# Second sequence's mLSTM memory: weighted scores turned by VectorE in 32x32 blocks and a DRAM round trip instead of by TensorE, with the heads interleaved

## The chip, the cores and the metric

The kernel runs on one core of a Trainium2 chip. The metric is the device time of one execution in microseconds (us). A core has several engines that run their own instruction streams side by side: TensorE (PE in the profile, with PEld for its weight loads), VectorE (DVE), ScalarE (ACT), GpSimd (POOL) and SyncE (SP), which here does little but issue DMA transfers. Each stream has a fixed order, set when the kernel is built; an instruction that waits holds up all behind it on its engine. Engines wait for each other through semaphores.

## The reference

One encoder layer is applied to two sequences of 512 tokens with 1024 channels, `x_prompt` (sequence 0) and `x_sample` (sequence 1), each on its own:

```python
def encoder_layer(x, ...):
    x = x + 0.5 * swiglu(rms_norm(x, ffn1_norm), ...)
    h = rms_norm(x, mix_norm)
    aq, ak, av, mq, mk, mv, gate_pre, o_pre, g_att, g_mlstm = split(h @ w_in)
    att = gqa_block_attention(aq, ak, av)
    mem = mlstm_bidirectional(mq, mk, mv, gate_pre, mlstm_gate_bias, o_pre, mlstm_head_norm)
    merged = sigmoid(g_att) * (att @ w_up_att) + sigmoid(g_mlstm) * (mem @ w_up_mlstm)
    x = x + merged @ w_out
    return x + 0.5 * swiglu(rms_norm(x, ffn2_norm), ...)

def mlstm_direction(q, k, v, logi, logf):      # 4 heads of 128 channels; run forward and backward
    ...
        S_qk = einsum('bhtd,bhsd->bhts', qc, kc) * exp(D - m_t[..., None])
        num = einsum('bhts,bhse->bhte', S_qk, vc) + ...
        den = sum(S_qk, axis=-1) + ...
        h = num / maximum(abs(den), exp(-m_t))[..., None]
```

The sum of the two directions is normalized over a head's 128 channels, scaled and gated by `sigmoid(o_pre)`.

## The kernel before

All is float32; a product is three TensorE matmuls of float32r parts: high x high, high x low, low x high (`split`, L715 and L716, makes the parts: ScalarE copies the high one, VectorE subtracts for the low one). After the first feed-forward network, `mix(s, ...)` does the token mixing of sequence s: attention, the mLSTM memory, the merge and the output projection.

The chunked recurrence is computed as one 512x512 matrix of weighted scores per head, both directions in it. For head h:

- `mem_head(h)`: for each of 4 row blocks of 128 queries, three score matmuls into PSUM (L1241), 5 exponentials of 128x128 on ScalarE (L1255; 20 a head) whose rows come from DRAM (`mem_rows`, L1064), a multiplication with a row sum on VectorE (L1257), and, after the denominators (L1261 to L1263), a scaling by them on ScalarE and VectorE (L1268 to L1271). The result `Ts[i][0]` has queries on partitions and keys along the free axis.
- `mem_out(h)`: the product with V needs keys on partitions. So for each of 4 key blocks j, four 128x128 transposes on TensorE (L1283; 16 a head, 64 a sequence) go into a PSUM bank, `split` makes high and low parts in SBUF, and three matmuls (L1291) add into the bank `po` of [channels, queries]. Then square (L1294, ScalarE), gate multiplication (L1296), `block_sums` (L225: VectorE's STREAM_TRANSPOSE, which turns each 32x32 block on its own), a fold matmul (L232), a reciprocal root by small VectorE steps (L235 to L241), spreading (L258), the final multiplication (L1302) and `split` into `mem`.

Other units of work lie between the heads as cover: `mem_qk(h, j)` (query and key projection of a later head), `att_gate` and `mem_gate(d)` (projections of the sigmoid gates, 24 matmuls each on L833; ScalarE's L866 empties the PSUM bank, of which this pool, `mm`, has three), `merge_att(d)` (12 matmuls). `go` runs units and loads the weights of the following ones ahead: sequence 1 reads them from DRAM, where sequence 0 parked them (`w<-wpark`, L293, two SyncE transfers of 512 KB a unit, into a pool of 4 slots). `queue` holds the units that `fill` lets out. The transposed parts, exponentials and other 128x512 work tiles come from one pool (`T2`, tag t2).

Every instruction gets a priority at the place in the code where it is written (`shifted(n)` moves it by n); a scheduler sets each engine's order from these when the kernel is built. In sequence 1 the heads ran one after the other: `mem_head(h)`, one or two units, `mem_out(h)`, more units; after the last head all eight `mem_gate`, then eight `merge_mem`, then the output projection.

Of the kernel before, what the change touches and what calls it, by code (L numbers as in the profile page):

```python
# [8 lines left out]
F32 = mybir.dt.float32  # L9
F32R = mybir.dt.float32r  # L10
I32 = mybir.dt.int32
AF = mybir.ActivationFunctionType
# [4 lines left out]
P = 128  # L17
S = 512
D = 1024
KD = D // P  # L20
# [6 lines left out]
def encoder(ctx, tc, I, outs):  # L27
    nc = tc.nc
    cpool = ctx.enter_context(tc.tile_pool(name="cpool", bufs=1))
    dpool = ctx.enter_context(tc.tile_pool(name="dpool", bufs=1, space=bass.MemoryType.DRAM))  # L30
    apool = ctx.enter_context(tc.tile_pool(name="apool", bufs=7))
    wpool = ctx.enter_context(tc.tile_pool(name="wpool", bufs=3))
# [9 lines left out]
    def nm(s):  # L42
        n_id[0] += 1
        return f"{s}_{n_id[0]}"

    @contextmanager
    def shifted(n):

        tc.cur_priority += n
        yield  # L50
        tc.cur_priority -= n
# [8 lines left out]
    def T2(dtype=F32, tag="t2"):  # L60
        if tag in ("eb", "ac"):
            i = boxes[tag]
            boxes[tag] += 1
            return boxes["tile"][:, i % 4 + (4 if tag == "ac" else 0), :]
        if tag == "R":
            return spool.tile([P, S], dtype, tag="R", bufs=2, name=nm("R"))
        n = {"t2": 11, "f2": 4}[tag]
        return tpool.tile([P, S], dtype, tag=tag, bufs=n, name=nm(tag))
# [41 lines left out]
    def PO():  # L110
        return po_.tile([P, S], F32, tag="o", name=nm("pso"))
# [4 lines left out]
    def PT():  # L116
        return pt.tile([P, S], F32, tag="t", name=nm("pst"))
# [16 lines left out]
    def A(shape, dtype=F32, name="a"):  # L134
        return apool.tile(shape, dtype, tag="a", name=nm(name))
# [85 lines left out]
    def block_sums(t, tag="f2"):  # L221

        row = spool.tile([P, 64], F32, tag="row", bufs=1, name=nm("row"))
        q = T2(F32, tag)
        nc.vector.transpose(q, t)  # L225
        nc.vector.tensor_reduce(row[:, 0:16], q.rearrange("p (n j) -> p n j", j=32), axis=AX.X, op=ALU.add)
        return row

    def block_rstd(row, n, keep=lambda i: i):

        p = PT()
        keep(nc.tensor.matmul(p[:, 0:16], fold, row[:, 0:16], start=True, stop=True))  # L232
        V = nc.vector
        a, y, u = [row[:, 16 * i:16 * i + 16] for i in (1, 2, 3)]
        V.tensor_scalar(a, p[:, 0:16], 1.0 / n, EPS, op0=ALU.mult, op1=ALU.add)  # L235
        V.tensor_scalar(u.bitcast(I32), a.bitcast(I32), 1, None, op0=ALU.logical_shift_right)
        V.tensor_scalar(y.bitcast(I32), u.bitcast(I32), -1.0, 1597463007.0, op0=ALU.mult, op1=ALU.add)
        for _ in range(3):
            V.scalar_tensor_tensor(u, y, -0.5, y, op0=ALU.mult, op1=ALU.mult)
            V.tensor_tensor(u, u, a, op=ALU.mult)  # L240
            V.scalar_tensor_tensor(y, u, 1.5, y, op0=ALU.add, op1=ALU.mult)  # L241
        return y
# [13 lines left out]
    def spread_rows(r16, R):  # L256

        nc.vector.transpose(R.rearrange("p (n j) -> p n j", j=32), r16.unsqueeze(2).to_broadcast([P, 16, 32]))  # L258
        return R
# [48 lines left out]
    V_ = nc.vector  # L308
# [404 lines left out]
    def split(src, hi, lo, eng=None):  # L713

        nc.scalar.activation(hi, src, AF.Copy)  # L715
        (eng or V_).tensor_tensor(lo, src, f(hi), op=ALU.subtract)  # L716
# [3 lines left out]
    HM, DM = 4, 128  # L720
# [50 lines left out]
    def go(*units):  # L771
        for load, comp in units:
            held.append((comp, load()))
            while len(held) > ahead[0]:
                c, w = held.pop(0)
                c(w)
# [64 lines left out]
    def mix(s, xh, xl, early=None, extra=None, after=None):  # L841
# [3 lines left out]
        queue = []  # L845

        def fill(n):
            go(*queue[:n])
            del queue[:n]

        def F2(dtype=F32):
            return T2(dtype, "f2")
# [10 lines left out]
        def gate_of(t, p):  # L863
            if not s:
                V_.tensor_tensor(t, p, R[s], op=ALU.mult)
            nc.scalar.activation(t, t if not s else p, AF.Tanh, scale=0.5)  # L866

        def win_cols(c0, done):
            return proj(win_v[:, :, c0:c0 + P], ("in", c0), xsrc, KD, done)
# [128 lines left out]
        def mem_values():  # L998
            def done(pvv):
                vm = A([P, 2, 4, S], F32R, "Vm")  # L1000
                for b in range(4):
                    nc.scalar.activation(vm[:, 0, b, :], pvv[b], AF.Copy, scale=rcol(b))
                    rest(vm[:, 1, b, :], pvv[b], b, f(vm[:, 0, b, :]))
                Vm.append(vm)
            return tok_proj(xh, xl, [(1792, 512)], 2, done, (MM, MM, MM, PO))
# [3 lines left out]
        def mem_qk(h, j):  # L1009
            def done(pp):  # L1010
                if j == 0 and not s:
                    t = wpool.tile([P, 4, S], F32R, tag="w8", bufs=4, name=nm("qk"))
                    qks[h] = [t[:, i] for i in range(4)]
                elif s:
                    t = wpool.tile([P, 2, S], F32R, tag="wr", bufs=4, name=nm("qk"))
                    qks.setdefault(h, []).extend(t[:, i] for i in range(2))
                t = pp
                if not s:
                    t = F2()
                    V_.tensor_tensor(t, pp, R[s], op=ALU.mult)  # L1020
                split(t, *qks[h][2 * j:2 * j + 2])
            return win_cols((768, 1280)[j] + h * P, done)

        ogs = {}
# [136 lines left out]
        for h in range(HA):  # L1161
            nxt = []
# [43 lines left out]
        def merge_att(d):  # L1206
            def done(pu):
                V_.scalar_tensor_tensor(mg[:, d, :], mg[:, d, :], 1.0, pu, op0=ALU.add, op1=ALU.mult)
            return up_unit(0, d, att, done)
# [3 lines left out]
        def mem_gate(d):  # L1213
            def done(pp):
                t = ths[d] = T2()
                gate_of(t, pp)
            return win_cols(3856 + d * P, done)
# [11 lines left out]
        mem = A([P, HM, 2, S], F32R, "mem")  # L1229

        def mem_head(h):
# [39 lines left out]
                    V_.tensor_scalar(tf[:, up_], tb[:, up_], rb, None, op0=ALU.mult)  # L1271
            return Ts

        def mem_out(h, Ts):
            vm = Vm[0]
            po = PO()
            hs_ = slice(h * P, (h + 1) * P)
            turned = []
            for j in range(4 + 1):
                if j < 4:  # L1280
                    p = PT()
                    for i in range(4):
                        nc.tensor.transpose(p[:, i * P:(i + 1) * P], Ts[i][0][:, j * P:(j + 1) * P], ident)  # L1283
                    ph, pl = T2(F32R), T2(F32R)
                    split(p, ph, pl)
                    turned.append((j, ph, pl))
                if j >= 1:
                    t, ph, pl = turned.pop(0)
                    with shifted(15):
                        for n, (a, b) in enumerate(((0, ph), (1, ph), (0, pl))):  # L1290
                            nc.tensor.matmul(po, vm[:, a, t, hs_], b, start=(t == 0 and n == 0),  # L1291
                                             stop=(t == 3 and n == 2))
            h2 = T2()
            nc.scalar.activation(h2, po, AF.Square)  # L1294
            og = ogs[h]
            V_.scalar_tensor_tensor(og, og, 1.0, po, op0=ALU.add, op1=ALU.mult)  # L1296
            row = block_sums(h2)
            with shifted(60):
                rh = block_rstd(row, DM)
            with shifted(160):  # L1300
                Rh = spread_rows(rh, T2(F32, "f2"))
                V_.scalar_tensor_tensor(og, og, hn[:, h:h + 1], Rh, op0=ALU.mult, op1=ALU.mult)  # L1302
                split(og, mem[:, h, 0, :], mem[:, h, 1, :])

        for h in range(HM):
            Ts = mem_head(h)
            if h == 0:
                go(*mem_values())
            queue.append(merge_att(2 * h))
            if h == 0:  # L1310
                queue.append(merge_att(1))
            fill(1 + s)
            mem_out(h, Ts)
            if h + 2 < HM:
                queue.extend([att_gate(h + 6), mem_qk(h + 2, 0), mem_qk(h + 2, 1)])
            if h:
                queue.append(merge_att(2 * h + 1))
            fill(99)

        mh, ml = A([P, KD, S], F32R, "mh"), A([P, KD, S], F32R, "ml")  # L1320
        go(*[mem_gate(d) for d in range(KD)])
        go(*[merge_mem(d) for d in range(KD)])
        flush()
        yield None
# [22 lines left out]
    def busy(n, idle):  # L1347

        for _ in range(n):
# [3 lines left out]
    x2buf = [dpool.tile([P, KD, S], F32, name=f"x2buf{s}") for s in range(2)]  # L1353
    rbuf = [[[dpool.tile([P, 2, S], F32, name=f"rbuf{n}_{j}_{m}") for m in range(7)] for j in range(NF // 2)]
            for n in range(2)]
    xnbuf = dpool.tile([P, KD, S], F32, name="xnbuf")
    raws = [A([P, 4, D], F32, "raw")]
    x0r_ = A([P, KD, S], F32, "x0r")
# [288 lines left out]
    r = [None, None]  # L1647
# [213 lines left out]
```

## Time and profile before

| | |
|---|---|
| runs, us | 2044.56, 2046.38, 2044.59; median 2044.59 |
| profiled execution: own time / span, us | 2046.24 / 2044.5 |
| mean granted TensorE clock | 0.999 |
| TensorE busy, us (share of the span) | 2034.3 (100%) |
| VectorE / ScalarE / GpSimd busy, us | 1571.5 / 909.1 / 93.6 |
| DMA, mean | 218 GB/s, 445.38 MB |
| second sequence's memory: first transpose to last product matmul | 1208.3 to 1287.4 us |

Matmuls overlap their neighbours in the pipeline, so that the recorded duration of one (0.39 us for 128x512) is longer than the time from its start to the next one's. "Idle before" and the waits name the instruction that ended the idle time. A group row reads: line, engine, operation, output<-inputs, count, busy us, mean ns of one, idle time before.

### The profile page before, as it was taken

To read this page: it belongs to the slowest core of one execution; us is meant where nothing else is said; L and a number is where in the kernel's file an instruction comes from. 1 tells how busy PE (TensorE), PEld (TensorE's weight loads), DVE (VectorE), ACT (ScalarE), POOL (GpSimd) and SP (SyncE) were. 2 spreads that over 40 slices of the span, in tenths; PEclk is the share of its full clock that TensorE was granted. 3 is DMA by queue.
4 is the path that set the end of the run, shared out by engine and by line. 5 is a ranking of instruction groups with operands and counts; after the bars stand their busy time and mean duration, and the time that the engine had idled before them with its cause. 6 is when DMAs were issued, how large, how long until landed. Compare 5 with 4: busy or idle time off the path is not lost.

```text
span 2044.5 us, 26753 instructions
## 1 busy us (share of the span) xinstructions
PE 2034.3 (100%) x9313; PEld 1680.7 (82%) x9313; DVE 1571.5 (77%) x2780; ACT 909.1 (44%) x1655; POOL 93.6 (5%) x116
## 2 busy tenths in 40 slices
PE   9999999999999999999999999999999999999998
PEld 7888888888888888888888888888888888888887
DVE  7988888886797798786567756366788988786797
ACT  7644444443234577563325554144444444442224
POOL 0000000001003000100120000001000000000001
PEclk9999999999999999999999999999999999999999
DMA  9656566799766853868564345667655655699753
GB/s 308 199 172 224 172 213 187 236 338 362 270 215 223 293 173 130 284 211 292 188 195 139 114 152 169 226 202 225 192 190 181 207 170 180 203 347 341 275 198 119
DMA packets 314727, 445.38 MB, mean 218 GB/s; under 512 B 19848, under 2 KB 189920, under 8 KB 313312
## 3 DMA queue, kind: packets, MB, share of 16 engines
q1 hardware_dynamic: 312512, 437.69, 63.8%
q0 software_dynamic: 1920, 5.72, 0.9%
q8 instruction: 73, 1.20, 0.2%
q14 instruction: 62, 0.51, 0.1%
q10 hardware_dynamic: 160, 0.27, 0.0%
HBM read 284.06 MB, written 159.55 MB: 217 GB/s over the span
## 4 chain that ended last, share of the span: by engine, by line
PE 96%; DVE 2%; ACT 1%; DMA 1%; issue 0%; SPq 0%; DVEq 0%; ACTq 0%
PE mm L833 15%; PE pst L374 12%; PE pso L374 12%; PE mm L374 10%; PE mm L632 8%; PE pss L374 6%; PE mm L820 5%; PE pst L632 4%; PE pss L632 4%; PE mm L800 4%; PE pso L632 3%; PE pso L1121 1%; PE pss L1094 1%; PE pst L1110 1%; PE pso L1291 1%; PE pss L1241 1%
## 5 line engine op out<-in xcount | busy, mean ns | idle before, releaser
L374 PE MATMUL pst<-xc,w 128*128 128x512 f32 x1056 | 253.7, 389 | 0.0
L374 PEld LDWEIGHTS pst<-xc,w 128*128 128x128 f32 x1056 | 198.2, 188 | 41.2
L374 PE MATMUL mm<-xc,w 128*128 128x512 f32 x972 | 229.7, 390 | 0.4 <-ACT f L382 0.4
L374 PEld LDWEIGHTS mm<-xc,w 128*128 128x128 f32 x972 | 182.0, 188 | 38.4 <-ACT f L382 0.8
L632 PE MATMUL mm<-rt,w 128*128 128x512 f32 x765 | 178.7, 389 | 0.0
L833 PE MATMUL mm<-xh,w 128*128 128x512 f32 x560 | 176.9, 392 | 0.0
L632 PEld LDWEIGHTS mm<-rt,w 128*128 128x128 f32 x765 | 143.5, 188 | 29.8
L332 ACT ACTIVATE w<-t 128x512 fp32r<-128x512 f32 x176 | 106.6, 627 | 135.6 <-issue 63.1
L333 DVE TENSOR_TENSOR w<-t,w 128x512 fp32r<-128x512 f32 x176 | 117.8, 687 | 42.9 <-ACT w L332 41.2
L374 PE MATMUL pss<-xc,w 128*128 128x512 f32 x528 | 126.8, 389 | 0.0
L374 PE MATMUL pso<-xc,w 128*128 128x512 f32 x528 | 126.8, 389 | 0.0
L374 PE MATMUL pso<-xc,f 128*128 128x512 f32 x528 | 126.8, 389 | 0.0
L833 PEld LDWEIGHTS mm<-xh,w 128*128 128x128 f32 x560 | 104.9, 188 | 21.9
L374 PEld LDWEIGHTS pss<-xc,w 128*128 128x128 f32 x528 | 99.1, 188 | 20.6
L374 PEld LDWEIGHTS pso<-xc,w 128*128 128x128 f32 x528 | 99.1, 188 | 20.6
L374 PEld LDWEIGHTS pso<-xc,f 128*128 128x128 f32 x528 | 99.1, 188 | 20.6
L820 PE MATMUL mm<-xh,w 128*128 128x512 f32 x336 | 113.4, 400 | 0.0
L833 PE MATMUL mm<-xl,w 128*128 128x512 f32 x280 | 109.6, 391 | 0.0
L715 ACT ACTIVATE w<-wr 128x512 fp32r<-128x512 f32 x72 | 45.1, 632 | 136.7 <-PE pso L632 71.2
L278 ACT ACTIVATE w<-wr 128x1024 fp32r<-128x1024 f32 (+1 forms) x64 | 65.3, 1029 | 79.1 <-issue 23.7
L279 DVE TENSOR_TENSOR w<-wr,w 128x1024 fp32r<-128x1024 f32 (+1 forms) x64 | 79.7, 1247 | 26.5 <-ACT w L278 15.7
L715 ACT ACTIVATE w<-t 128x512 fp32r<-128x512 f32 x82 | 51.8, 632 | 107.6 <-PE pst L632 62.5
(444 smaller groups left out, 4068.7 us busy)
## 6 DMA issues: line engine op xcount, KB each, us to landing
rt<-rbuf SPq DMA_DIRECT2D x154, 512.0 KB, 5.5
wpark<-w SPq DMA_DIRECT2D x88, 512.0 KB, 3.8
w<-wpark SPq DMA_DIRECT2D x88, 512.0 KB, 4.4
wr<-in_ffn_w_gate_dram SPq DMA_DIRECT2D x62, 512.0 KB, 5.3
rbuf<-tab SPq DMA_DIRECT2D x102, 256.0 KB, 4.0
wr<-in_ffn_w_up_dram SPq DMA_DIRECT2D x44, 512.0 KB, 4.5
rbuf<-f SPq DMA_DIRECT2D x72, 256.0 KB, 4.0
wr<-in_w_in_dram SPq DMA_DIRECT2D x36, 512.0 KB, 5.7
```

The costliest lines, as they stand in the source:

```text
L278: pin(nc.scalar.activation(hi, raw, AF.Copy))
L279: pin(lo_eng.tensor_tensor(lo, raw, f(hi), op=ALU.subtract))
L332: pin(nc.scalar.activation(t[:, 0], src, AF.Copy))
L333: pin(V_.tensor_tensor(t[:, 1], src, f(t[:, 0]), op=ALU.subtract))
L374: nc.tensor.matmul(p, a[:, k, :], xt[:, b, k, :], start=(first and k == 0 and i == 0), stop=(k == HK_ - 1 and i == 2), skip_group_check=True)
L632: nc.tensor.matmul(p, u[:, a, d * P:(d + 1) * P], r[:, b, ts], start=(first and q == 0 and k == 0), stop=(q == len(us) - 1 and k == 2), sk ...
L715: nc.scalar.activation(hi, src, AF.Copy)
L800: nc.tensor.matmul(p[b][:, :N], a[:, k, bs], w_[:, kl, :], start=(k == 0 and i == 0), stop=(k == KD - 1 and i == 2))
L820: pin(nc.tensor.matmul(p[0], a[:, k, :], b, start=(k == 0 and i == 0), stop=(k == n - 1 and i == 2)))
L833: nc.tensor.matmul(p, a[:, k, :], b, start=(k == 0 and i == 0), stop=(k == n - 1 and i == 2))
L1094: pin(nc.tensor.matmul(p, qT[:, h, b * P:(b + 1) * P], kv[:, hk * 2 + j, :], start=(j == 0), stop=(j == 1)))
L1110: pin(nc.tensor.transpose(p[:, b * P:(b + 1) * P], Ps[b][:, kb * P:(kb + 1) * P], ident))
```

## The change

Only sequence 1 changes (`if s`). `mem_blocks(h, Ts)` turns the weighted scores by 8 VectorE STREAM_TRANSPOSEs of 128x256 (L1279) into two tiles `q` of the `wr` pool (named `qt`), and writes them by 8 SyncE transfers of 128 KB in runs of 512 bytes (L1283) into one of two DRAM buffers `tbuf`. `mem_out` reads key block j back by one transfer of 256 KB (L1295) into a t2 tile, which `split` takes instead of a PSUM bank; TensorE's transposes are gone there. The columns come back in another order, so ScalarE copies `po` with the order undone (L1314) ahead of the square (L1317); L1318 and L1324 are the former L1296 and L1302, L1308 the former L1291, and L1299 the former L1283 (sequence 0 only).

`mem_head(h + 1)` and its blocks now stand ahead of `mem_out(h)`. The queue's order is another one: `mem_gate(0)` to `mem_gate(2)` are put in during head 2 and so run ahead of and between the products of heads 2 and 3. Head 2's query and key parts lie in a part of `mem` instead of the `wr` pool.

```diff
@@ -1012,7 +1012,7 @@
                     t = wpool.tile([P, 4, S], F32R, tag="w8", bufs=4, name=nm("qk"))
                     qks[h] = [t[:, i] for i in range(4)]
                 elif s:
-                    t = wpool.tile([P, 2, S], F32R, tag="wr", bufs=4, name=nm("qk"))
+                    t = mem[:, 2 + j] if h == 2 else wpool.tile([P, 2, S], F32R, tag="wr", bufs=4, name=nm("qk"))
                     qks.setdefault(h, []).extend(t[:, i] for i in range(2))
                 t = pp
                 if not s:
@@ -1271,16 +1271,33 @@
                     V_.tensor_scalar(tf[:, up_], tb[:, up_], rb, None, op0=ALU.mult)
             return Ts
 
+        def mem_blocks(h, Ts):
+
+            q = [wpool.tile([P, 8, 4, 32], F32, tag="wr", bufs=4, name=nm("qt")) for _ in range(2)]
+            for i in range(4):
+                for g in range(2):
+                    V_.transpose(q[g][:, :, i, :],
+                                 Ts[i][0][:, g * 256:(g + 1) * 256].rearrange("p (n m) -> p n m", m=32))
+            for g in range(2):
+                for a in range(4):
+                    nc.sync.dma_start(tbuf[h % 2][8 * g:8 * g + 8, :, a, :].rearrange("n r x -> r n x"),
+                                      q[g][32 * a:32 * a + 32].rearrange("r n i m -> r n (i m)"))
+            return h % 2
+
         def mem_out(h, Ts):
             vm = Vm[0]
             po = PO()
             hs_ = slice(h * P, (h + 1) * P)
             turned = []
             for j in range(4 + 1):
-                if j < 4:
+                if j < 4 and s:
+                    p = T2()
+                    nc.sync.dma_start(p, tbuf[Ts][4 * j:4 * j + 4].rearrange("c r a x -> (c r) (a x)"))
+                elif j < 4:
                     p = PT()
                     for i in range(4):
                         nc.tensor.transpose(p[:, i * P:(i + 1) * P], Ts[i][0][:, j * P:(j + 1) * P], ident)
+                if j < 4:
                     ph, pl = T2(F32R), T2(F32R)
                     split(p, ph, pl)
                     turned.append((j, ph, pl))
@@ -1291,8 +1308,13 @@
                             nc.tensor.matmul(po, vm[:, a, t, hs_], b, start=(t == 0 and n == 0),
                                              stop=(t == 3 and n == 2))
             h2 = T2()
+            og = ogs[h]
+            if s:
+                rows_ = T2()
+                nc.scalar.activation(rows_.rearrange("p (i a m) -> p i a m", i=4, a=4),
+                                     po.rearrange("p (a i m) -> p i a m", i=4, a=4), AF.Copy)
+                po = rows_
             nc.scalar.activation(h2, po, AF.Square)
-            og = ogs[h]
             V_.scalar_tensor_tensor(og, og, 1.0, po, op0=ALU.add, op1=ALU.mult)
             row = block_sums(h2)
             with shifted(60):
@@ -1302,7 +1324,24 @@
                 V_.scalar_tensor_tensor(og, og, hn[:, h:h + 1], Rh, op0=ALU.mult, op1=ALU.mult)
                 split(og, mem[:, h, 0, :], mem[:, h, 1, :])
 
-        for h in range(HM):
+        if s:
+            at = mem_blocks(0, mem_head(0))
+            go(*mem_values())
+            queue.extend([merge_att(0), merge_att(1)])
+            fill(99)
+            for h in range(HM):
+                if h + 1 < HM:
+                    nxt = mem_blocks(h + 1, mem_head(h + 1))
+                mem_out(h, at)
+                at = nxt
+                if h + 2 < HM:
+                    queue.extend([mem_qk(h + 2, 0), mem_qk(h + 2, 1), merge_att(2 * h + 2), att_gate(h + 6)])
+                    queue.append(merge_att(2 * h + 3))
+                elif h == 2:
+                    queue.extend([merge_att(6), merge_att(7)])
+                    queue.extend(mem_gate(d) for d in range(3))
+                fill(99)
+        for h in range(HM if not s else 0):
             Ts = mem_head(h)
             if h == 0:
                 go(*mem_values())
@@ -1318,7 +1357,7 @@
             fill(99)
 
         mh, ml = A([P, KD, S], F32R, "mh"), A([P, KD, S], F32R, "ml")
-        go(*[mem_gate(d) for d in range(KD)])
+        go(*[mem_gate(d) for d in range(3 * s, KD)])
         go(*[merge_mem(d) for d in range(KD)])
         flush()
         yield None
@@ -1353,6 +1392,7 @@
     x2buf = [dpool.tile([P, KD, S], F32, name=f"x2buf{s}") for s in range(2)]
     rbuf = [[[dpool.tile([P, 2, S], F32, name=f"rbuf{n}_{j}_{m}") for m in range(7)] for j in range(NF // 2)]
             for n in range(2)]
+    tbuf = [dpool.tile([16, 32, 4, P], F32, name=f"tbuf{i}") for i in range(2)]
     xnbuf = dpool.tile([P, KD, S], F32, name="xnbuf")
     raws = [A([P, 4, D], F32, "raw")]
     x0r_ = A([P, KD, S], F32, "x0r")
```

Three places of the built program. First TensorE. Before, head 3's product (`pso_11305`) ends in the last att_gate projections, and the mem_gates follow (`mm_11433` is mem_gate(0)):

```order
L1291 MATMUL pso_11305<-t_1487_11344,Vm_10597 128x512 x2
L833 MATMUL mm_11399<-att_9329,w_11288 128x512 x2
L1291 MATMUL pso_11305<-t_1488_11345,Vm_10597 128x512
L833 MATMUL mm_11399<-att_9329,w_11288 128x512 x4
L833 MATMUL mm_11416<-att_9329,w_11288 128x512 x12
L232 MATMUL pst_11361<-row_11357,fold 128x16
L833 MATMUL mm_11433<-xh_8370,w_11396 128x512
```

Now the end of head 2's product (`pso_11253`) is followed at once by mem_gate(3) (`mm_11555`), and mem_gate(0) to (2) (`mm_11398`, `mm_11495`, `mm_11525`) have run before:

```order
L833 MATMUL mm_11525<-xh_8372,w_11395 128x512
L1308 MATMUL pso_11253<-t_1469_11262,Vm_10617 128x512 x2
L1308 MATMUL pso_11253<-t_1470_11263,Vm_10617 128x512
L1308 MATMUL pso_11253<-t_1472_11271,Vm_10617 128x512 x2
L1308 MATMUL pso_11253<-t_1473_11272,Vm_10617 128x512
L1308 MATMUL pso_11253<-t_1475_11280,Vm_10617 128x512 x2
L1308 MATMUL pso_11253<-t_1476_11281,Vm_10617 128x512
L833 MATMUL mm_11555<-xh_8372,w_11492 128x512
```

So the gates moved from behind both products to between them. mem_gate(4) (`mm_11585`) likewise stands right behind the end of head 3's product (`pso_11425`).

ScalarE at the same place, before: head 3's square (L1294), then one gate's evacuation after the other:

```order
L715 ACTIVATE t_1487_11344<-pst_11339 128x512
L1294 ACTIVATE t_1489_11354<-pso_11305 128x512
L715 ACTIVATE mem_10410<-box_5274 128x512
L866 ACTIVATE t_1503_11458<-mm_11433 128x512
L866 ACTIVATE t_1506_11488<-mm_11463 128x512
```

and now: head 2's copy and square, mem_gate(0)'s evacuation, the split of head 3's reads (`t_1494`, `t_1497`, `t_1500`, `t_1503`), head 3's copy and square, mem_gate(1)'s evacuation:

```order
L1314 ACTIVATE t_1478_11291<-pso_11253 128x512
L1317 ACTIVATE t_1477_11290<-t_1478_11291 128x512
L866 ACTIVATE t_1492_11423<-mm_11398 128x512
L715 ACTIVATE t_1495_11428<-t_1494_11426 128x512
L715 ACTIVATE t_1498_11434<-t_1497_11432 128x512
L715 ACTIVATE mem_10412<-box_5276 128x512
L715 ACTIVATE t_1501_11443<-t_1500_11441 128x512
L715 ACTIVATE t_1504_11452<-t_1503_11450 128x512
L1314 ACTIVATE t_1507_11463<-pso_11425 128x512
L1317 ACTIVATE t_1506_11462<-t_1507_11463 128x512
L866 ACTIVATE t_1516_11520<-mm_11495 128x512
```

mem_gate(0)'s and mem_gate(1)'s evacuations moved behind the copies that read the two products.

SyncE, before: weight loads only (`w` parked weights, `wr` raw ones of the output projection):

```order
L293 DMA w_11097<-wpark_7753 128x1024 x2
L293 DMA w_11288<-wpark_7935 128x1024 x2
L293 DMA w_11396<-wpark_8048 128x1024 x2
L271 DMA wr_11862<-in_w_out_dram 128x8x128
L271 DMA wr_11867<-in_w_out_dram 128x8x128
L293 DMA w_11413<-wpark_8070 128x1024 x2
```

and now: head 3's eight writes (`tbuf_260`), head 2's reads 1 to 3 (`tbuf_259`), loads between them:

```order
L1283 DMA tbuf_260<-qt_11235 32x8x128 x4
L1283 DMA tbuf_260<-qt_11236 32x8x128 x4
L1295 DMA t_1468_11260<-tbuf_259 128x512
L293 DMA w_11552<-wpark_8216 128x1024
L293 DMA w_11582<-wpark_8252 128x1024
L1295 DMA t_1471_11269<-tbuf_259 128x512
L293 DMA w_11582<-wpark_8252 128x1024
L271 DMA wr_11899<-in_w_out_dram 128x8x128
L1295 DMA t_1474_11278<-tbuf_259 128x512
```

Head 2's reads moved in behind head 3's writes. A little further on stand head 3's reads, the last of them behind the loads of `w_11612`:

```order
L1295 DMA t_1494_11426<-tbuf_260 128x512
L1295 DMA t_1497_11432<-tbuf_260 128x512
L1295 DMA t_1500_11441<-tbuf_260 128x512
L293 DMA w_11612<-wpark_8288 128x1024 x2
L1295 DMA t_1503_11450<-tbuf_260 128x512
```

The fourth read moved behind a weight load, the first three stand together ahead of it.

## The prediction

> **What bounds the kernel now.** I read the page first (busy time by engine), then TensorE's waits, then busy time by windows over the stage that the change touches, then single lines and stretches of the timeline there.
>
> The page's first lines (busy us, share of the span, instructions):
>
> ```profile
> span 2044.5 us, 26753 instructions
> PE 2034.3 (100%) x9313; PEld 1680.7 (82%) x9313; DVE 1571.5 (77%) x2780; ACT 909.1 (44%) x1655; POOL 93.6 (5%) x116
> ```
>
> All waits of TensorE in the span (us in total, times, longest):
>
> ```profile
> PE pst L1350 <- DVE xc L1433: 1.6, 1, 1.6
> PE pst L1370 <- DMA raw<-in_x_prompt_dram: 0.5, 1, 0.5
> PE mm L374 <- ACT f L382: 0.4, 1, 0.4
> PE pst L1370 <- ACT tab L1498: 0.2, 1, 0.2
> ```
>
> Busy us in windows of 20 us around the second sequence's memory (PE, PEld, DVE, ACT, POOL, granted clock, DMA share, GB/s):
>
> ```profile
> 1200.00:1220.00 20.00, 20.00 (x97) 16.51 (x96) 8.39 (x13) 10.36 (x28) 0.00 (x0) 1.00 0.41 142
> 1220.00:1240.00 20.00, 20.00 (x97) 16.25 (x96) 15.35 (x50) 8.03 (x18) 0.00 (x0) 1.00 0.57 182
> 1260.00:1280.00 20.00, 19.94 (x97) 16.21 (x96) 15.51 (x58) 11.61 (x32) 0.00 (x0) 1.00 0.66 201
> ```
>
> TensorE is the bound, and in the stage of the change it never waits. So every TensorE instruction removed there is time gained, every wait that the change creates on TensorE is time lost, and no slack behind it can take a loss back: it is busy to the end. The forecast is one difference: transposes removed, minus new waits.
>
> The profiled execution took 2046.24 us, 1.7 more than its span; the runs' median is 2044.59. I add the difference to the median.
>
> **What is removed.** 64 of the 128 transposes on L1283 (second sequence). First their group in 1180 to 1300 us, then two stretches of TensorE's timeline:
>
> ```profile
> L1283 PE MATMUL pst<-ident,t 128*128 128x128 f32 x64 | 9.0, 274 | 0.0
> ...
> 1208.30 1.04 PE L1283 MATMUL pst<-ident,t 128*128 128x128 f32 x8
> 1209.10 0.94 PE L833 MATMUL mm<-att,w 128*128 128x512 f32 x3
> ...
> 1235.11 0.60 PE L1283 MATMUL pst<-ident,t 128*128 128x128 f32 x4
> 1235.46 0.48 PE L1291 MATMUL pso<-t,Vm 128*128 128x512 f32 x1
> 1235.78 0.49 PE L1283 MATMUL pst<-ident,t 128*128 128x128 f32 x3
> ```
>
> Instructions overlap, so I count from start to start: 8 transposes take 0.80, and 4 take 0.35 with the matmul behind them starting its successor 0.32 later instead of 0.23, so 0.44. Both come to 0.11 us each: 64 x 0.11 = **7.1 us removed** (the group's busy 9.0 also counts the overlap).
>
> Here a rule of the Trainium skill speaks against the change: "VectorE: DVE Perf Modes", Rules for kernel authors, says to turn 128x128 on TensorE where PSUM will do as destination, and VectorE turns 32x32 blocks only; The three transpose paths gives 390 ns for TensorE's. By that figure 64 removals would be worth an estimated 25 us, and the sum below would end at 2036; the trace has 270 ns for one and 0.11 in a row, so the measurement decides. The rule's direction agrees with my sum.
>
> **What is added away from TensorE.** Per head: 8 VectorE block transposes of 128x256, 8 SyncE writes of 128 KB, 4 reads of 256 KB, one more ScalarE copy (L1314). Prices from these rows (the timeline, then groups in 1180 to 1300 us, then the page's transfers with median us to landing):
>
> ```profile
> 1211.53 2.53 PE L1291 MATMUL pso<-t,Vm 128*128 128x512 f32 x10
> 1213.90 2.43 PE L833 MATMUL mm<-att,w 128*128 128x512 f32 x10
> 1214.10 0.60 ACT L1294 ACTIVATE t<-pso 128x512 f32<-128x512 f32 x1 [1.63 <-PE pso L1291]
> 1214.59 1.57 ACT L1255 ACTIVATE t<-box,st 128x128 f32<-128x128 f32 x5
> 1214.73 0.69 DVE L1296 SCALAR_TENSOR_TENSOR box<-box,pso 128x512 f32<-128x512 f32 x1 [1.43 <-ACT t L1294]
> 1215.33 0.70 DVE L225 STREAM_TRANSPOSE f<-t 128x512 f32<-128x512 f32 x1
> 1215.96 0.65 DVE L1208 SCALAR_TENSOR_TENSOR mg<-mg,mm 128x512 f32<-128x512 f32 x1
> 1219.99 0.92 SPq L1064 DMA_DIRECT2D box<-ebuf  x2
> 1265.36 1.08 ACT L715 ACTIVATE t<-pst 128x512 fp32r<-128x512 f32 x2
> 1266.01 0.30 PEld L1291 LDWEIGHTS pso<-t,Vm 128*128 128x128 f32 x2 [0.38 <-ACT t L715]
> 1275.83 1.28 ACT L1255 ACTIVATE t<-box,st 128x128 f32<-128x128 f32 x4
> 1282.01 0.31 DVE L1269 SCALAR_TENSOR_TENSOR t<-t,dn,t 128x128 f32<-128x128 f32 x1
> ...
> L715 ACT ACTIVATE mem<-box 128x512 fp32r<-128x512 f32 x4 | 2.5, 631 | 13.2 <-DVE box L1302 13.2
> L866 ACT ACTIVATE mg<-mm 128x512 f32<-128x512 f32 x3 | 1.8, 599 | 5.3 <-PE mm L833 3.8 <-PE mm L820 1.5
> ...
> t<-kept SPq DMA_DIRECT2D x44, 256.0 KB, 2.9
> ...
> box<-ebuf SPq DMA_DIRECT2D x16, 256.0 KB, 5.0
> ...
> f<-x2buf SPq DMA_DIRECT2D x8, 256.0 KB, 3.9
> ```
>
> From them: a 128x512 matmul 0.227 ((2.43 − 0.39) / 9, ten on L833, the last lasting 0.39); last matmul of a product to ScalarE 0.43 (the last of L1291 begins at 1211.53 + 2.53 − 0.39 = 1213.67, ScalarE at 1214.10); ScalarE 128x512 back to back 0.49; one of the exponentials 0.295 ((1.57 − 0.39) / 4); a VectorE STREAM_TRANSPOSE 128x512 0.63, so 0.35 for 128x256 by half and a start; a split's first part from SBUF 0.63; ScalarE's end to TensorE's weight load 0.05; one SyncE issue 0.46 (0.92 for two). VectorE gains 32 x 0.35 = 11.2 and ScalarE 4 x 0.49 = 2.0 us; in the windows both have more than that idle (VectorE 8.4 to 15.5 of 20), so as totals they cost nothing. SyncE gains 48 issues, 22 us over a stage of about 90, nothing as a total either. A read's landing no row has: 2.9 to 5.0 by the nearest (256 KB into SBUF); I take 3.9, a read from a DRAM buffer with VectorE's result in it, as here.
>
> What costs is the position in each engine's fixed order. Heads are counted 0 to 3.
>
> *Early heads.* Head 0's product waits for a low part of a split queued on VectorE behind head 1's 8 block transposes (8 x 0.35 = 2.8, mostly covered by 6 to 11 matmuls): 0.7. Head 2's scores follow mem_qk(2,1)'s last matmul by two others only, and the split needs 0.43 + 0.60 and VectorE's part: 0.6. A fold matmul and a read that waits for a free t slot: 0.9 together. I take **2.2**, ends 0.5 and 4.
>
> *Head 2's product (the wait I am surest of in kind, not in size).* On SyncE its reads j = 1 to 3 stand behind head 3's 8 writes, which wait for head 3's blocks. From the last matmul of head 1's product: 0.43, two ScalarE steps 0.98, 20 exponentials 5.9; from the last exponential's end to the last scaling as before 5.2 (1277.11 to 1282.32); 8 block transposes 2.8; 8 writes 3.7; that is 19.0. The read lands 3.9 later, ScalarE 0.63, 0.05: 23.6. TensorE has 87 matmuls in between, 19.7: it waits 3.9. Reads j = 2 and 3 stand three places further on SyncE each (1.4 against 0.7 of matmuls): 1.4 more, and 0.3 for the last low part. **5.6**, ends 2.7 and 8.5.
>
> *mem_gate(3) and mem_gate(4).* The mm pool has three banks. mem_gate(3) takes mem_gate(0)'s, which ScalarE's L866 empties; but L866 now stands behind L1314 and L1317 of head 2, which wait for that head's last matmul, and TensorE runs mem_gate(3) right behind that matmul. So 0.43 + 0.49 + 0.49 + 0.60 + 0.05 − 0.23 = **1.8**. mem_gate(4) meets the same behind head 3: **1.8**. (Before, all eight gates ran after the heads, so that no L866 stood behind a product.)
>
> *Head 3's last read.* On SyncE it stands behind the two loads of w_11612, which wait until TensorE has freed a weight slot, five matmuls ahead of the product's part that needs the read. So 0.43 + 2 x 0.46 + 3.9 + 0.63 + 0.05 − 5 x 0.23 = 4.8, and 0.3 for the low part: **5.1**, ends 4.1 and 6.2.
>
> **Sum:** 2.2 + 5.6 + 1.8 + 1.8 + 5.1 = 16.5 lost, 7.1 gained: +9.4, so 2044.6 + 9.4 = **2054.0 us**. With all low ends +3.8 (2048.4), with all high ends +15.2 (2059.8). The last three terms alone, which hang on fixed positions and not on a race, are 8.7 and outweigh the gain.
>
> **Rivals.**
>
> *The round trip is hidden (faster).* Only the 7.1 us go: 2037.5. The place is head 2's reads: the chain of 23.6 would have to be under 19.7, as with block transposes and writes that take 2.6 instead of 6.5, and then ScalarE's copy for mem_gate(3) would also have to come before head 2's product. Against it: the waits on L866 and behind w_11612 are set by order, whatever the speed of the chain. For it: VectorE's and ScalarE's idle time above. It wins if the waits together stay under 3 us. 0.07, partial forms included.
>
> *Gain and loss cancel (same).* By 0.2% (4.1 us), about what a measurement of this kernel tells from no change, 2040.5 to 2048.7 is no change. That needs waits of 3 to 11.2 us: the early ones and head 2's near their low ends, landing at 2.9. About 2047. 0.18.
>
> *The clock drops in a new wait (slower still).* The end and the start of the span (windows as above, and TensorE's first and last rows):
>
> ```profile
> 2036.00:2042.20 6.20, 1.73 (x15) 1.53 (x13) 4.01 (x11) 3.41 (x10) 0.00 (x0) 0.97 0.70 260
> 2042.20:2044.50 2.30, 0.00 (x0) 0.00 (x0) 0.00 (x0) 0.00 (x0) 0.00 (x0) 0.50 0.19 70
> ...
> 1.63 2.93 PE L1350 MATMUL pst<-xc 128*128 128x512 f32 x6 [1.63 <-DVE xc L1433]
> ...
> 2036.49 1.24 PE L648 MATMUL mm<-w,rt 128*128 128x256 f32 x9
> ```
>
> TensorE's last matmul ended at 2037.73; a mean of 0.97 to 2042.2 and 0.50 behind it put the halving near 2041.8, 4.1 us later. At the start six matmuls took 2.93, 0.43 a step instead of 0.23, so a slow stretch of 3 to 7 us costs 1.5 to 3.5. Two of my waits (3.9 and 4.8) lie at that length. If one drops the clock: 2054.0 + 2.5 = 2056.5. 0.2. The Trainium skill, "TensorE: Matmul & The Clock Gate", Part 1, says the same thing with a figure of its own: half rate after an idle window of about 3.4 us, full again after as long busy. By that rule both waits would drop the clock, an estimated 1.7 us each; the tail above agrees with a window of that order.
>
> *DMA crowding.* The stage's DMA share is 0.41 to 0.66 and gets 8 MB more in some 90 us, 89 GB/s beside 142 to 201. If reads land in 5.0 or later, the two long waits grow by 1.1 each: 2056.2; counted in with the forecast's upper part. 0.1.
>
> **How the numbers follow.** Forecast 0.45, clock 0.2, crowding 0.1, cancelling 0.18, hidden 0.07. Slower by over 0.2%: 0.75; within: 0.18; faster: 0.07. Range 2046.5 to 2062: below it lies the hidden case and a little of the cancelling one, above it two clock drops on top of high ends (15.2 + 3.5 gives 2063).
>
> **What would show it.** Right: TensorE's waits, none in the stage before, now some 16 us, the largest on ScalarE's L715 fed by reads of tbuf (head 2 j = 1, head 3 j = 3) and on L866 ahead of mem_gate(3) and (4); SyncE's reads issued right behind w_11612. TensorE busy down 7. Wrong: no wait on L715 over 2 us, or reads that land in under 2.5 us; block transposes much faster than 0.35, or writes issued faster than 0.46, which would shorten head 2's chain by up to 4; a granted clock under 1 in 1240 to 1300. The forecast is wrong above all if waits merge: a late head 2 pushes head 3's product back, so that its reads are long there by then, except the one behind w_11612.

## The result and the profile after

The changed kernel takes 2067.6 us in the median of four runs (2066.94 to 2069.68), the kernel before 2045.13 beside it: a ratio of 1.0111, 95% interval 1.0093 to 1.0128. So it is 22.5 us slower. The forecast was 9.4 slower with a range to 2062: the sign was right, the size was not, and the range was missed by 5.6 us. The profiled execution took 2066.94 us, its span 2065.1, 20.6 over the span before. Two executions measured with the experiments below, one of e2 (2536.83 us) and one of the kernel before beside it (4954.88 us), lie far above all others and are left out.

First the page of the changed kernel and all of TensorE's waits there:

```profile
span 2065.1 us, 26735 instructions
PE 2036.5 (99%) x9249; PEld 1678.1 (81%) x9249; DVE 1580.1 (77%) x2812; ACT 911.1 (44%) x1659; POOL 92.9 (5%) x116
...
PE pso L1308 <- ACT t L715: 15.1, 6, 5.4
PE mm L833 <- ACT t L866: 3.7, 2, 1.8
```

Two waits are new: the products (L1308) for the high parts of the reads, 15.1 us, and the gates (L833) for L866, 3.7. TensorE has 64 instructions fewer and is still busy 2.2 us longer, so it also ran slower somewhere. Windows of the stage (the granted clock is the third number from the right) show where:

```profile
1240.00:1260.00 20.00, 19.25 (x84) 15.21 (x85) 15.67 (x54) 9.29 (x25) 0.00 (x0) 1.00 0.88 256
1260.00:1280.00 20.00, 20.00 (x90) 16.40 (x88) 5.79 (x11) 4.76 (x12) 0.00 (x0) 1.00 0.64 213
1280.00:1300.00 20.00, 16.58 (x73) 12.95 (x71) 11.90 (x49) 7.57 (x21) 0.00 (x0) 1.00 0.78 241
1300.00:1320.00 20.00, 12.64 (x32) 8.57 (x33) 8.97 (x23) 5.05 (x9) 0.00 (x0) 0.57 0.65 197
1320.00:1340.00 20.00, 12.72 (x46) 9.52 (x45) 8.07 (x22) 4.68 (x9) 0.00 (x0) 0.74 0.31 106
```

Up to 1296 us little is lost. In the 40 us from 1300 to 1340 TensorE works 25, and the clock is at 0.57 and 0.74. The places, on TensorE's timeline:

```profile
1296.19 0.39 PE L833 MATMUL mm<-xh,w 128*128 128x512 f32 x1
1300.04 1.22 PE L1308 MATMUL pso<-t,Vm 128*128 128x512 f32 x3 [3.46 <-ACT t L715]
1304.57 1.65 PE L1308 MATMUL pso<-t,Vm 128*128 128x512 f32 x3 [3.31 <-ACT t L715]
1308.40 1.65 PE L1308 MATMUL pso<-t,Vm 128*128 128x512 f32 x3 [2.18 <-ACT t L715]
1311.88 0.80 PE L833 MATMUL mm<-xh,w 128*128 128x512 f32 x1 [1.83 <-ACT t L866]
...
1321.90 1.07 PE L1308 MATMUL pso<-t,Vm 128*128 128x512 f32 x4
1328.41 1.65 PE L1308 MATMUL pso<-t,Vm 128*128 128x512 f32 x3 [5.44 <-ACT t L715]
1331.89 0.79 PE L833 MATMUL mm<-xh,w 128*128 128x512 f32 x1 [1.83 <-ACT t L866]
```

These are head 2's blocks 1 to 3, mem_gate(3), head 3's block 3 and mem_gate(4): the places that the prediction named. On SyncE (start, time for all of a row) and ScalarE at the same time:

```profile
1291.51 4.56 SPq L1283 DMA_DIRECT2D tbuf<-qt  x8
1296.17 0.42 SPq L1295 DMA_DIRECT2D t<-tbuf  x1
1296.64 0.92 SPq L293 DMA_DIRECT2D w<-wpark  x2
1297.60 0.43 SPq L1295 DMA_DIRECT2D t<-tbuf  x1
1298.07 0.47 SPq L293 DMA_DIRECT2D w<-wpark  x1
1298.59 0.51 SPq L271 DMA_DIRECT2D wr<-in_w_out_dram  x1
1299.19 1.35 SPq L1295 DMA_DIRECT2D t<-tbuf  x1
...
1322.09 0.80 SPq L293 DMA_DIRECT2D w<-wpark  x2
1322.94 0.42 SPq L1295 DMA_DIRECT2D t<-tbuf  x1
...
1299.35 0.63 ACT L715 ACTIVATE t<-t 128x512 fp32r<-128x512 f32 x1 [10.86 <-DMA t<-tbuf]
1303.88 0.63 ACT L715 ACTIVATE t<-t 128x512 fp32r<-128x512 f32 x1 [3.90 <-DMA t<-tbuf]
1307.72 0.63 ACT L715 ACTIVATE t<-t 128x512 fp32r<-128x512 f32 x1 [3.20 <-DMA t<-tbuf]
1327.72 0.63 ACT L715 ACTIVATE t<-t 128x512 fp32r<-128x512 f32 x1 [7.39 <-DMA t<-tbuf]
```

Head 2's read 1 is issued behind head 3's eight writes and is there 3.2 us later. Read 2 has two 512 KB loads between it and read 1, and takes 6.3; read 3 has two more, and takes 8.5. Head 3's last read, behind two loads, takes 4.8.

From start to start on TensorE, less 0.23 a matmul, the stage loses: in the early heads 2.8; before and between head 2's blocks 3.6 + 3.85 + 3.15 = 10.6; to mem_gate(3) 2.8 and to mem_gate(4) 2.8 (each 1.83 of wait, 0.6 for three matmuls at half clock, and 0.4 by which the last of them lasts longer than its step); ahead of head 3's block 3 5.6; and by slow matmuls of mem_gate(3) and (4) 2.9 and 1.8. That is 29.3; less the 7.1 removed, 22.2, beside 20.6 by the spans and 22.5 by the medians.

### The profile page after: what moved, and what is told of

Its sections match the earlier page's. It is cut to its first block, busy times and chain, and to the rows that moved or that the text cites. A ratio compares the mean times of both kernels' runs of the same rounds, so it can differ in the third digit from the quotient of the medians.

```text
span 2065.1 us, 26735 instructions
## 1 busy us (share of the span) xinstructions
PE 2036.5 (99%) x9249; PEld 1678.1 (81%) x9249; DVE 1580.1 (77%) x2812; ACT 911.1 (44%) x1659; POOL 92.9 (5%) x116
## 4 chain that ended last, share of the span: by engine, by line
PE 95%; DVE 2%; DMA 1%; ACT 1%; issue 0%; SPq 0%; DVEq 0%; ACTq 0%
PE mm L833 14%; PE pso L374 12%; PE pst L374 12%; PE mm L374 11%; PE mm L632 8%; PE pss L374 6%; PE mm L820 5%; PE pst L632 4%; PE pss L632 4%; PE mm L800 4%; PE pso L632 3%; PE pso L1121 1%; PE pss L1094 1%; PE pst L1110 1%; DMA t<-tbuf 1%; PE pso L1308 1%
## 5 line engine op out<-in xcount | busy, mean ns | idle before, releaser
L833 PE MATMUL mm<-xh,w 128*128 128x512 f32 x560 | 180.7, 398 | 3.7 <-ACT t L866 3.7
L833 PEld LDWEIGHTS mm<-xh,w 128*128 128x128 f32 x560 | 106.7, 191 | 27.3 <-ACT t L866 4.9
L374 PEld LDWEIGHTS pso<-xc,w 128*128 128x128 f32 x528 | 99.1, 188 | 20.6
L374 PEld LDWEIGHTS pss<-xc,w 128*128 128x128 f32 x528 | 99.1, 188 | 20.6
L833 PE MATMUL mm<-xl,w 128*128 128x512 f32 x280 | 111.1, 397 | 0.0
L279 DVE TENSOR_TENSOR w<-wr,w 128x1024 fp32r<-128x1024 f32 (+1 forms) x64 | 79.7, 1246 | 27.3 <-ACT w L278 16.5
```

Of the source, the lines that this page charges most:

```text
L279: pin(lo_eng.tensor_tensor(lo, raw, f(hi), op=ALU.subtract))
L374: nc.tensor.matmul(p, a[:, k, :], xt[:, b, k, :], start=(first and k == 0 and i == 0), stop=(k == HK_ - 1 and i == 2), skip_group_check=True)
L833: nc.tensor.matmul(p, a[:, k, :], b, start=(k == 0 and i == 0), stop=(k == n - 1 and i == 2))
```

## The experiments

All are compared with runs of the kernel before on the same chip. **Are the reads late because of what stands among them on SyncE?** The first experiment moves loads only, here those of the gates' weights (`behind` is `mem_gate(d)`'s load); the compute engines keep their order there but for one split on VectorE and a few matmuls behind head 2's product:

```diff
+            def behind():
+                if s and d >= 5:
+                    with tc.issue_after(lastread[3 if d == 7 else 2]):
+                        return load()
+                return load()
```

The output projection's first three loads are put behind head 3's last read in the same way.

> The changed kernel, TensorE's, VectorE's and ScalarE's order kept: on SyncE only, the loads of w_11552, w_11582, w_11612 and of the first output weights come behind the last read of the head that they stood among. Theory (the reads land late because 512 KB loads are queued between them and ahead of the last one): head 2's first read lands about 3 us after its issue as before, the next two within 1 us of each other instead of 4.5 and 3.8, head 3's last read is not late; with no wait over 3.6 us left the clock does not drop, or for a few us. Lost: early heads 2.8, head 2 about 4, the two gate waits 3.7, against 7.1 gained: about 2048.5. Rival (the reads of tbuf are slow in themselves, 512-byte writes and their read-back, whatever stands between): landings stay at 6 to 8 us and the time above 2060. Forecast as it stood (all landings 3.9): 2051 to 2054.

Measured: 2052.52 us in the median of four runs (2051.97 to 2054.98), ratio 1.0036 (1.0022 to 1.0050), 15.1 less than the changed kernel. SyncE and ScalarE there, and TensorE's waits:

```profile
1294.87 1.40 SPq L1303 DMA_DIRECT2D t<-tbuf  x3
...
1298.62 0.63 ACT L715 ACTIVATE t<-t 128x512 fp32r<-128x512 f32 x1 [10.77 <-DMA t<-tbuf]
1299.44 0.63 ACT L715 ACTIVATE t<-t 128x512 fp32r<-128x512 f32 x1 [0.19 <-DMA t<-tbuf]
1301.64 0.63 ACT L715 ACTIVATE t<-t 128x512 fp32r<-128x512 f32 x1 [1.57 <-DMA t<-tbuf]
...
PE pso L1316 <- ACT t L715: 5.0, 3, 3.3
PE mm L833 <- ACT t L866: 3.7, 2, 1.8
```

The three reads now are there within 3.0 us of each other instead of 8.4, and head 3's last read is waited for no more. The theory holds in the main. The time is 4.0 us above its number and lies where I had put the forecast with all landings at 3.9: read 3 was 2.2 behind read 2, and the one wait of 3.3 still halved the clock for 10 us (what that costs is asked below).

**Why do the reads stand there at all?** A read can be issued when its tile is free, and the tile comes from the t2 pool. The next experiment changes where the tile comes from, and nothing else in the code; the order that the scheduler then builds is another one on TensorE, ScalarE, VectorE and SyncE:

```diff
-                    p = T2()
+                    p = T2(F32, "f2")
```

> The changed kernel with one word changed: the tile that a read of tbuf fills comes from the f2 pool (4 buffers) instead of the t2 pool (11 buffers, which also holds exponentials, split parts, the copies of the product and the gates' results). Theory (the reads are late on SyncE because their tiles are late: with t2 exhausted a read can only be issued when a buffer falls free, by then behind the next head's writes and weight loads; mem_gate's L866 is late for the same reason, its t2 tile): the four reads of a head stand together on SyncE ahead of the next head's writes, no wait on L866, no wait of TensorE over 2 us, clock 1. The 7.1 us of transposes less 2.8 us of early waits and 1 to 3 of new small ones: 2041.5 to 2044, faster than the kernel before by 1.5 to 4 us. Rival (the round trip costs what it saves, wherever its tiles lie): 2045.5 or more.

Measured: 2041.42 us, ratio 0.9979 (0.9970 to 0.9988): this word turns 22 us of loss into 3.9 of gain. TensorE's waits, SyncE with the last two heads' writes and reads (`f` is the read's tile now), ScalarE with head 2's four splits:

```profile
PE pst L1389 <- DVE xc L1473: 1.6, 1, 1.6
PE pss L1241 <- ACT mem L715: 0.7, 1, 0.7
PE pso L1308 <- DVE t L716: 0.5, 1, 0.5
...
1251.60 4.04 SPq L1283 DMA_DIRECT2D tbuf<-qt  x8
1255.76 1.00 SPq L1064 DMA_DIRECT2D box<-ebuf  x2
1256.86 4.22 SPq L1295 DMA_DIRECT2D f<-tbuf  x4
1261.13 12.38 SPq L293 DMA_DIRECT2D w<-wpark  x8
1281.78 3.91 SPq L1283 DMA_DIRECT2D tbuf<-qt  x8
1285.87 0.84 SPq L1295 DMA_DIRECT2D f<-tbuf  x2
...
1269.72 0.62 ACT L715 ACTIVATE t<-f 128x512 fp32r<-128x512 f32 x1
1270.72 0.62 ACT L715 ACTIVATE t<-f 128x512 fp32r<-128x512 f32 x1
1276.24 0.63 ACT L715 ACTIVATE t<-f 128x512 fp32r<-128x512 f32 x1 [4.91 <-PE pso L1308]
1278.60 0.62 ACT L715 ACTIVATE t<-f 128x512 fp32r<-128x512 f32 x1
```

(The 1.6 us is at the kernel's start and was there before.) Head 2's four reads stand together behind their own writes, 25 us ahead of head 3's, and ScalarE waits for none of them. The wait on L866 is gone with them: its tile, too, was one of t2. The reads are not quick here: issue to landing has a median of 6.5 us (2.7 to 8.8), over the 3.9 that the prediction took. They are early, and then it does not matter.

**Tile or queue?** Reads issued from GpSimd, with tiles from t2 and from f2:

```diff
-                    nc.sync.dma_start(p, tbuf[Ts]...)
+                    nc.gpsimd.dma_start(p, tbuf[Ts]...)
```

> The changed kernel with the reads of tbuf issued by GpSimd instead of SyncE; tiles from t2 as in the change. Theory of e5 (the tile is late): some reads still wait for a tile, but nothing else is queued behind them and they are behind no write or load, so that most of the loss goes: 2044 to 2048. If SyncE's queue alone is the cause (and not the tiles): 2042 or less, as good as e5. If the queue is no cause: above 2060.

> Both edits of e5 and e6. If the tiles are the cause and SyncE's order only its effect, it is e5 within 2 us: 2041 to 2044. If SyncE's queue costs by itself, it is 2 to 4 us faster than e5.

Measured: 2045.61 (ratio 1.0002, 0.9993 to 1.0010) and 2043.19 (0.9987, 0.9978 to 0.9996). Off SyncE the reads no longer have foreign work ahead of them, and most of the loss goes without an edit to the tiles; but with free tiles SyncE is as good or better (2041.42). The Trainium skill ("DMA: Bandwidth & Descriptors", Issuing engines are not separate DMA queues) says that transfers started by different engines interleave on the same 16 engines; that fits here: with own tiles the reads land no sooner from GpSimd (median 7.2 us) than from SyncE (6.5).

**Earlier reads by priority alone**, tiles from t2:

```diff
-                    nc.sync.dma_start(p, tbuf[Ts]...)
+                    with shifted(-300 if Ts >= 0 else 0):
+                        nc.sync.dma_start(p, tbuf[Ts]...)
```

> The changed kernel with the reads of tbuf given a priority 300 earlier. SyncE then issues each read as soon as its tile is free, ahead of the next head's writes and of weight loads, and the scheduler spreads all four products between other matmuls (head 2's blocks now have 12 to 15 matmuls between them). Theory (position on SyncE is the cause, the round trip itself is short enough to hide): no wait of TensorE on reads over 1 us, clock 1, the 7.1 us of transposes come through less 1 to 4 us of small waits: 2039 to 2043, faster than the kernel before. Rival (a DRAM round trip costs more than the transposes wherever it stands, by DMA traffic and by the copies on ScalarE): no faster than 2045.

Measured: 2047.27, ratio 1.0010 (1.0000 to 1.0019). The clock held, but products and scores still waited for tiles and splits:

```profile
PE pso L1309 <- ACT t L715: 4.3, 3, 2.1
PE pss L1241 <- DVE t L1257: 1.8, 1, 1.8
PE pso L1309 <- DVE t L716: 1.7, 1, 1.7
```

So the expected gain over the kernel before did not come: an earlier place on SyncE alone, with tiles from t2, repairs 20 us, not the rest. **Is it the moved gates?**

```diff
-                    queue.extend(mem_gate(d) for d in range(3))
...
-        go(*[mem_gate(d) for d in range(3 * s, KD)])
+        go(*[mem_gate(d) for d in range(KD)])
```

> The changed kernel with one part undone: all eight mem_gates run after the heads, as before the change; reads from t2 as in the change. Theory (t2's exhaustion makes the reads late, whoever fills the time): head 2's reads still stand behind head 3's writes, and head 3's product now follows head 2's with less work between, so its waits come in place of the gate waits: 2062 to 2069, no better than the changed kernel by more than 5 us. Rival (mem_gate between the products, with its L866 and its weight loads among the reads, is the cause): below 2055.

Measured: 2064.71, ratio 1.0090 (1.0076 to 1.0104). The part undone changes 3 us of 22; the reads of head 2 still stand behind head 3's writes, with read 1 issued at 1295.18 against 1296.17. The moved gates are not the cause.

**What does the clock cost?** Spare matmuls are to keep TensorE busy in its four long waits (13, 13, 13 and 21 of them; the lines that fix their order are left out here):

```diff
+                        if fill_:
+                            spare = PT()
...
+                                for n in range(fill_):
+                                    m_ = nc.tensor.matmul(spare, vm[:, 0, 0, hs_], vm[:, 0, 1, :], ...)
```

> The changed kernel, with spare matmuls into an unused PSUM bank put into TensorE's four long waits: 13 each (3.0 us at 0.227) ahead of key blocks 1, 2 and 3 of head 2's product, 21 (4.8 us) ahead of block 3 of head 3's. They delay nothing if the reads set the time there, since the waits are 3.6, 3.6, 3.2 and 5.6 us long. Theory (two causes: the waits themselves and a halved clock, which the excess of about 0.2 us on each of some 30 matmuls between 1301 and 1336 us puts at 6.3 us): the granted clock stays near 1 and the time falls by 5 to 6.5 us, to about 2061.5. Rival (the waits are everything, the lower clock costs nothing because TensorE waits anyway): within 1 us of the changed kernel's 2067.6. Second rival (spare work disturbs the reads or the order): slower.

Measured: 2067.1 (2062.89 to 2069.16), ratio 1.0101 (1.0084 to 1.0118). The clock in 1300 to 1320 rose from 0.57 to 0.91, in 1320 to 1340 only from 0.74 to 0.83, and the median stayed. Why, ScalarE's row for head 3's last read tells:

```profile
1300.00:1320.00 20.00, 17.01 (x63) 12.46 (x64) 9.73 (x24) 5.39 (x9) 0.00 (x0) 0.91 0.66 200
1327.89 0.63 ACT L715 ACTIVATE t<-t 128x512 fp32r<-128x512 f32 x1 [8.48 <-DMA t<-tbuf]
```

It comes at 1327.89, with the slow clock at 1327.72. The two loads ahead of that read began 1.2 us earlier (1320.90 against 1322.09), but took 2.10 us to issue instead of 0.80; so what TensorE gained in between it waited for there. My 5 to 6.5 us did not come: I had added up slow matmuls without asking what ended behind them. But the test is a partial one. The clock still fell at 1313.81 for 3.4 us and, behind head 3's product, at 1330.87 for 6.8 us (17.1 and 10.2 in the changed kernel), so the second slow stretch was not taken away; and one run of the four, 2062.89, lies 4 us under the others, so the gain may come in some executions. In e2 no read is late behind its slow stretch, so there the same edit should pay:

> The kernel of e2 (loads behind the reads, 2053.0) with 13 spare matmuls (3.0 us) in head 2's 3.5 us wait, in which e2's clock fell to half for 10 us and 22 matmuls took 0.43 instead of 0.23 us. Theory (here no read is late behind that wait, so that the clock is on the path): the granted clock stays 1 and the time falls by 3.5 to 4.5 us, to about 2049. Rival (as in e1, transfers set the time there and the clock is hidden): within 1 us of e2.

Measured: 2051.87, ratio 1.0033 (1.0020 to 1.0046), 0.65 below e2, a difference that the intervals do not separate from none. Window 1300 to 1320 of e2, then of this run:

```profile
1300.00:1320.00 20.00, 15.77 (x53) 11.40 (x53) 12.07 (x27) 8.04 (x15) 0.00 (x0) 0.74 0.60 213
```

```profile
1300.00:1320.00 20.00, 15.25 (x61) 10.47 (x62) 13.76 (x35) 8.61 (x15) 0.00 (x0) 1.00 0.75 264
```

The clock is full, mem_gate(4) starts 1.6 us earlier by the traces (1317.04 against 1318.61), and the 3.5 to 4.5 us did not come: mem_gate(3) starts no earlier (1305.87 against 1305.80), as the slow matmuls ahead of it lay beside read 3 here too. So the clock's own price in e2 is some 1.6 us by the traces and not shown by the run times; in the changed kernel it stays open.

One experiment told nothing about its question. The gates' tanh was given an earlier priority:

> The changed kernel with one edit in ScalarE's order: the tanh that empties a mem_gate bank (L866) has a priority 300 earlier, so that mem_gate(0) and (1) are emptied ahead of the copies of heads 2 and 3. Theory (the two 1.83 us waits on L866 are that order alone, and TensorE is the bound, so that they come off one to one, with the share of them that was run at half clock): 3.7 to 5 us less, about 2063. Rival (the next read is late anyway, the wait only moves): head 3's last read is then waited for 1.8 longer and only the second gate's 1.8 comes off, about 2065.5.

Measured: 2067.68, ratio 1.0109 (1.0094 to 1.0124). All engines' instructions come in the order of the changed kernel, one for one, so that L866 is not behind the copies by its priority. That it waits for a t2 tile is not shown here; e5, where L866 is no more late, bears it out. As a time this run is a second measurement of the changed kernel.

**Is more to be had?** e5 with two edits of order:

```diff
-   queue.extend([mem_qk(h + 2, 0), mem_qk(h + 2, 1), merge_att(2 * h + 2), att_gate(h + 6)])
+   queue.extend([att_gate(h + 6), mem_qk(h + 2, 0), mem_qk(h + 2, 1), merge_att(2 * h + 2)])
...
+                  with shifted(40):
                     V_.transpose(q[g][:, :, i, :], ...)
```

> e5 (reads' tiles from f2, 2041.4) with two edits of order: att_gate ahead of mem_qk in the queue, so that 24 more matmuls stand between a head's blocks and its product, and the block transposes 40 later in priority, so that VectorE does a split that TensorE waits for first. e5's TensorE still lost 3.5 us in small waits ahead of products, scores and folds; if half of them go: 2039 to 2040.5. Rival (they are spread and belong to other steps, or DMA landings set them): within 1 us of e5.

Measured: 2040.43, ratio 0.9978 (0.9969 to 0.9987) beside 0.9979 for e5: no difference that these runs show. Both beat the kernel before and the changed one.

## Why the prediction came out as it did

*Bound and gain: right.* TensorE was the bound without slack, and 64 transposes at 0.11 us, 7.1, fit e5: 7.1 less some 3.5 of small waits on its TensorE is 3.6, measured 3.9.

*Prices of the added work: near, but for the writes.* Eight block transposes took 2.72 us (2.8 forecast), the copy in ScalarE 0.60 (0.49), head 3's eight writes 4.56 (3.7). That they cost nothing as totals fits e5.

*The places: right.* Early heads lost 2.8 (2.2); TensorE waited 1.83 at each of the two gates (1.8, which I took for the whole loss; with the slow matmuls ahead it was 2.8); head 3's last read cost 5.6 (5.1), behind w_11612; head 2's read 1 was waited for 3.6 (3.9). That last agreement is partly luck: transposes and writes together took 0.6 longer than priced (7.1 from the first transpose to the read's issue, against 6.5), and the read landed 0.7 sooner (3.2 against 3.9).

*The step that failed: the spacing of head 2's reads 2 and 3.* I put it at three issues of SyncE, 1.4 us, and let each transfer land in 3.9 from whatever median row I found. They took 6.3 and 8.5, as four 512 KB loads were queued with them, and the term was 10.6 instead of 5.6: 5.0 of the 12.8 by which the losses counted above (29.3) exceed my 16.5. e2 shows it: without those loads the three reads come within 3.0 us. The rival of crowded transfers had the mechanism, but with 1.1 us for each wait, from an average share of the stage where the queue at that place was needed.

*The rival that came true beside it: the clock.* I gave it a chance of 0.2 and 2.5 us, and in the sum itself nothing. It was at half for 17 us (1301.4 to 1318.4, from the mean of 0.84 in 1300 to 1302 and 0.89 in 1318 to 1320) and for 10 us (1325.3 to 1335.5), longer than the 3 to 7 of my row, which came from a stretch without new waits. Some 6 us of the 29 counted above, and so nearly half of the 12.8, are slow matmuls. How much of that would come off alone is open: e1 took the clock's loss away only in part, and in its trace the gain ended in a later wait for a read; e8 gained 1.6 us by the traces. That the reads come first is shown from the other side: in e5, where ScalarE waits for none of head 2's reads, the clock is at 1 through the whole stage.

*What I did not see: the pool.* I read the reads' place from the order and took it for a property of the round trip. It hung on the t2 pool, in which reads, splits, exponentials and gate results share 11 tiles: with tiles of f2 (four buffers) for the reads, e5 gains 3.9. The pool is not the only way to it, as an earlier priority (e4) or another queue (e6) repairs 20 to 22 of the 22.5 with tiles from t2; but none of the runs with tiles from t2 was faster than the kernel before. The rival "hidden round trip" comes true in e5, 3.9 of its 7.1 us, and its condition as I wrote it (a shorter chain) was the wrong one.

## What to carry to other kernels

Where a transfer stands in its queue can be set by when its destination tile comes free: ask which pool the tile is from and who else holds it. A round trip may be slow and still be free if it is issued early, so price its position, and price its landing from what is queued beside it there, not from a median over the kernel. Several losses in a row are not a sum: slow matmuls beside a late transfer need not cost anything, and before an experiment on the one is believed, its trace must show that the one is really gone.

## What the runs showed of the hardware

The clock can fall after shorter waits than the 4.1 us read off the kernel's end. In e7 TensorE waited 1.89 us, and the clock was at half for 3.4 us:

```profile
1212.12 0.50 PE L1308 MATMUL pso<-t,Vm 128*128 128x512 f32 x1 [1.89 <-ACT t L715]
...
1209.32:1212.74 3.42, 1.53 (x8) 0.93 (x7) 2.29 (x10) 0.63 (x1) 0.00 (x0) 1.00 1.01 401
1212.74:1216.15 3.41, 3.41 (x10) 2.64 (x9) 1.67 (x8) 0.63 (x1) 0.00 (x0) 0.50 0.74 296
```

Not the length of the wait alone counts, but where it lies. Within each trace the clock changes only at whole steps of 3.41 us from one change to the next: in the changed kernel it is at half from 1301.38 to 1318.45 and from 1325.27 to 1335.51, five steps and three. In the stages of all runs it fell nine times, each time behind a step in which TensorE was busy for 0 to 1.67 us (1.53 above, 1.22 and 1.10 in the changed kernel), and came back each time behind the first step without idle time; the step from 1311.62 to 1315.03, with 3.15 us busy, did not bring it back. The limit is not sharp: steps with 1.67 us busy in e4 and 1.50 in e6 left the clock at 1. In e6 a wait of 2.69 us lay across two steps (1.50 and 2.64 us busy) and left it at 1. After the wait of 3.46 in the changed kernel the clock fell 4.8 us past the wait's start, at the end of such a step, with work already under way. The Trainium skill ("TensorE: Matmul & The Clock Gate", Part 1) has half rate after about 3.4 us idle and a window that runs on by itself; the second fits these steps, the first is no safe limit here (1.89 us were enough).
